# Four norm factors of a two-layer decoder kernel: from per-column sums and a spreading product to one product with a matrix of ones

## The chip, the cores and the metric

The kernel runs on 1 core of one Trainium2 chip. The metric is the time of one execution on the device in microseconds (us); smaller is better. The chip gave the kernel before 2523.98 us as the median of 3 runs (2523.86 to 2524.05). Beside these runs there is one profiled execution, whose trace is read here; L-numbers in it are lines of the kernel before.

## The reference

A decoder with two layers works on a residual stream h of 256 tokens by 2048 features in float32. Layer 0 has a dilated sliding-window attention, layer 1 a sparse attention with shared keys and values. What surrounds the change is the second half of each layer:

```python
def rmsnorm(x, g):
    xf = x.astype(jnp.float32)
    y = xf * lax.rsqrt(jnp.mean(xf * xf, axis=-1, keepdims=True) + NORM_EPS)
    return (y * g.astype(jnp.float32)).astype(x.dtype)

for i in range(DEPTH):                      # DEPTH = 2
    hn = rmsnorm(h, attn_norm_g[i])
    h = h + attention_i(hn)                 # two different mixers
    hn = rmsnorm(h, mlp_norm_g[i])
    h = h + jnp.square(jax.nn.relu(hn @ mlp_w1[i])) @ mlp_w2[i]
    gate = jax.nn.sigmoid(rmsnorm(h, ple_norm_g[i]) @ ple_w_gate[i])
    h = h + (p[i] @ ple_w_proj[i]) * gate
return rmsnorm(h, final_norm_g)
```

Every norm needs one number for each token: the reciprocal root of the mean square over 2048 features. The change is about how this number is made for four of the seven norms: the one before the MLP and the one before the gate, in both layers.

## The kernel before

**Tiles.** The stream is kept feature-major: 16 tiles `x[k]` of 128 features (partitions) by 256 tokens (columns). A product's stationary operand is a block of a weight matrix, its moving operand a tile of the stream. float32 accuracy is had from products of rounded parts: a weight chunk `raw` (128x1024 float32, 512 KB) is loaded by SP (L184), rounded to float32r by ScalarE (`whi`, L196), and what the rounding left is made by VectorE (`wlo`, L202). The stream's tiles are split in the same way into 512 columns: 256 of the rounded part, 256 of the rest. `mm_tile` then issues two products for a block of weights: `whi` with all 512 columns (L318) and `wlo` with the first 256 (L319).

**Order.** The order of all engines is written out by hand. `Program.run` goes over the weight chunks. For each chunk it issues the load up to seven chunks ahead (4 buffers of `raw`), the rounding four ahead (6 buffers of `whi`), the rest `wlo` three ahead (5 buffers); then it lets each open generator take one step (`advance`); then it issues the chunk's products; then it starts what has yielded the word `"tensor"`, which so stands behind the chunk's products. A `quad` is eight chunks that fill four PSUM banks (512 features of the output); a chunk in it is eight pairs of products. Two groups of four banks are used in turn, `mm` and `at`.

**The norm's factor.** The squares of the 16 tiles are summed into `acc` (128 partitions by 256 tokens). What is left is to sum `acc` over the partitions, and to have the result's reciprocal root on all 128 partitions, since it scales tiles whose partitions are features. `Norm.factor` starts behind chunk 4 of the first quad that uses the norm (`hooks`) and takes four steps:

- `column` (L234): for each half of the tokens a product with `acc` as stationary operand and one column of ones as moving operand. It gives the sums with tokens on partitions, 128x2.
- `root` (L240, L241): mean and epsilon on VectorE, the square root on ScalarE, both 128x2.
- `invert` (L247 to L253): a reciprocal, three operations that refine it, and two that multiply the identity with it, which gives `diag` (128x256). All on VectorE.
- `spread` (L257): a float32 product of a matrix of ones with `diag`, which puts the factors on all partitions; ScalarE copies them from PSUM to `sr` (L273).

Four norms go that way in the first quad of `mlp` (layers 0 and 1, scaled by `sr` at L461) and of the gate's quads in `ple` (L522). The norms before the two attentions use the same function with `roped=True`, and they also need the 128x2 column; the final norm calls `column`, `root`, `invert` and `spread` directly.

Of the kernel before, what the change touches and what calls it, by code (L numbers as in the profile page):

```python
# [10 lines left out]
F32 = mybir.dt.float32  # L11
F32R = mybir.dt.float32r
AF = mybir.ActivationFunctionType
ALU = mybir.AluOpType

P = 128
D = 2048
T = 256
KT = D // P
DH = 128  # L20
EPS = 1e-6
# [18 lines left out]
def f32(ap):  # L40
    return ap.bitcast(F32)
# [90 lines left out]
def kernel(ctx: ExitStack, tc: tile.TileContext, a: dict, out: bass.AP):  # L132
    nc = tc.nc
# [3 lines left out]
    const = ctx.enter_context(tc.tile_pool(name="const", bufs=1))  # L137
    xpool = ctx.enter_context(tc.tile_pool(name="x", bufs=1))
    stat = ctx.enter_context(tc.tile_pool(name="stat", bufs=2))
    tmp = ctx.enter_context(tc.tile_pool(name="tmp", bufs=2))  # L140
# [4 lines left out]
    cur = {}  # L145
# [10 lines left out]
    def bank():  # L156
        return pspool.tile([P, 512], F32, tag="mm", name="mm", bufs=4)

    def banks2():
        return pspool.tile([P, 2, 512], F32, tag="at", name="at", bufs=2)  # L160
# [5 lines left out]
    x = [xp[k // 2][:, k % 2 * T:(k % 2 + 1) * T] for k in range(KT)]  # L166
    ones = const.tile([P, P], F32, name="ones")
    nc.vector.memset(ones, 1.0)
    ident = const.tile([P, P], F32, name="ident")
    ropeC = const.tile([32, T], F32, name="ropeC")  # L170
    ropeS = const.tile([32, T], F32, name="ropeS")
# [34 lines left out]
    class Norm:  # L206
# [49 lines left out]
        def spread(self, ps):  # L256
            nc.tensor.matmul(ps[:, 128:128 + T], ones, self.diag, start=True, stop=True)  # L257
            return ps[:, 128:128 + T]

        def factor(self, roped=False):  # L260
            while self.done < KT:
                yield
            yield "tensor"
            ps = self.column([self.acc])
            yield
            self.root(ps)
            yield
            self.invert()
            yield "tensor"
            rp = self.spread(ps)  # L270
            yield
            r = stat.tile([P, T], F32, tag="sr", name="sr", bufs=1)
            nc.scalar.copy(r, rp)  # L273
            if roped:
                yield
                self.rc = stat.tile([P, T], F32, tag="rc", name="rc", bufs=1)
                self.rs = stat.tile([32, T], F32, tag="rs", name="rs", bufs=1)
                nc.vector.tensor_mul(self.rs, r[:32, :], ropeS)
                nc.vector.tensor_copy(self.rc, r)
                nc.vector.tensor_mul(self.rc[:32, :], r[:32, :], ropeC)  # L280
            self.r = r
# [39 lines left out]
    def sum_halves(ps):  # L321
        s = tmp.tile([P, T], F32, tag="es", name="es", bufs=4)
        nc.scalar.copy(s, ps[:, :T])  # L323
        t = tmp.tile([P, T], F32, tag="et", name="et", bufs=7)
        nc.vector.tensor_add(t, ps[:, T:], s)  # L325
        return t

    parity = [0]
# [123 lines left out]
    def mlp(layer, xg, norm, to, norm2):  # L452
        for b in range(NFB):
            h = [None] * 16
            for q in range(4):
                def done(f, ps, q=q, h=h):
                    t = sum_halves(ps)
                    yield
                    while norm.r is None:
                        yield  # L460
                    nc.vector.scalar_tensor_tensor(t, t, 0.0, norm.rb, op0=ALU.max, op1=ALU.mult)  # L461
                    yield
                    nc.scalar.activation(t, t, AF.Square)
                    ht = cur["h"].tile([P, 2 * T], F32R, tag="h", name="h", bufs=20)
                    yield from split_to(ht, t)
                    h[4 * q + f] = ht
                base = layer * 128 + (b * 4 + q) * 8
                quad(lambda c, base=base: a["w1"][base + c], KT, xg, done,
                     {4: [norm.factor]} if b == 0 and q == 0 else None, late=True)
            for q in range(4):  # L470
                def done(f, ps, q=q, b=b):
                    k = 4 * q + f
                    add_to_x(k, ps)
                    if b == NFB - 1:
                        yield
                        yield from renorm(k, G_PLE + layer, to, norm2)
                base = layer * 128 + (b * 4 + q) * 8
                quad(lambda c, base=base: a["w2"][base + c], 16, h, done, late=True)
# [10 lines left out]
    def ple(layer, pg, xg, norm, nxt, norm2, last):  # L489
        pj = [None] * KT  # L490

        def last_gate(ps):

            k = KT - 1
            prog.until(lambda: norm2.done == k)
            t = tmp.tile([P, T], F32, tag="et", name="et", bufs=7)
            nc.vector.tensor_mul(t, ps[:, :T], norm.rb)
            nc.scalar.activation(t, t, AF.Sigmoid)
            nc.scalar.activation(warm, ones[:, :1], AF.Sqrt)
            nc.vector.tensor_mul(t, t, pj[k])  # L500
            nc.vector.tensor_add(x[k], x[k], t)
            s = norm2.square(k, nc.vector)
            col = norm2.column([norm2.acc, s])
            norm2.root(col)
            nc.scalar.activation(x[k], x[k], AF.Identity, scale=gains[:, G_FIN, k:k + 1])
            norm2.invert()
            r = norm2.spread(col)
            for i, (k0, n) in enumerate([(0, 1), (1, 1)] + [(2 * j, 2) for j in range(1, KT // 2)]):
                y = xp[k0 // 2][:, k0 % 2 * T:(k0 % 2 + n) * T]
                y3 = y.rearrange("p (n t) -> p n t", t=T)  # L510
                nc.vector.tensor_mul(y3, y3, r[:, None, :].to_broadcast([P, n, T]))
                (nc.sync, nc.scalar)[i % 2].dma_start(out[:, k0 * T:(k0 + n) * T], y)
            return
            yield

        def gate_done(k, ps):
            t = sum_halves(ps)
            for _ in range(k % 4 // 2):
                yield
            while norm.r is None:  # L520
                yield
            nc.vector.tensor_mul(t, t, norm.rb)  # L522
            yield
            nc.scalar.activation(t, t, AF.Sigmoid)
            yield
            nc.vector.tensor_mul(t, t, pj[k])
            nc.vector.tensor_add(x[k], x[k], t)
            yield
            if last or k < 12:
                s = norm2.square(k)  # L530
                if last:
                    nc.scalar.activation(x[k], x[k], AF.Identity, scale=gains[:, G_FIN, k:k + 1])
                yield
                norm2.add(s)
            else:
                yield from renorm(k, G_KV, nxt, norm2)

        for q in range(4):
            def proj_done(f, ps, q=q):
                s = tmp.tile([P, T], F32, tag="es", name="es", bufs=4)  # L540
                nc.scalar.copy(s, ps[:, :T])
                t = cur["h"].tile([P, T], F32, tag="pj", name="pj", bufs=8)
                nc.vector.tensor_add(t, ps[:, T:], s)
                pj[4 * q + f] = t
                return
                yield
            quad(lambda c, q=q: a["w_proj"][layer * 4 + q], 2, pg, proj_done)
            hooks = {4: [norm.factor]} if q == 0 else {}
            if q == 3 and not last:
                for c in range(6):  # L550
                    hooks[c] = [lambda k=k: split_x(k, G_KV, nxt) for k in (2 * c, 2 * c + 1)]
            if q == 3 and last:
                for f in range(4):
                    single(lambda c, f=f: a["w_gl"][2 * f + c], xg,
                           (lambda ps, k=12 + f: gate_done(k, ps)) if f < 3 else last_gate,
                           ring=lambda: banks2()[:, 0, :], one_half=f == 3)
            else:
                quad(lambda c, q=q: a["w_gate"][layer * 32 + q * 8 + c], KT, xg,
                     lambda f, ps, q=q: gate_done(4 * q + f, ps), hooks)
# [21 lines left out]
    def start_x(k):  # L581
        return split_x(k, G_ATTN, x_a0)
# [117 lines left out]
    hooks = {c: [lambda k=k: start_x(k) for k in (2 * c + 2, 2 * c + 3)] for c in range(7)}  # L700
# [3 lines left out]
    for h in range(HA):  # L704
        for i in range(6):
            single(lambda c, h=h, i=i: a["w_qk"][(h * 6 + i) * 2 + c], x_a0,
                   lambda ps, h=h, i=i: qk_done(h, i, ps),
# [418 lines left out]
    for h in range(HB):  # L1126
# [4 lines left out]
        if h:  # L1131
            prog.op(lambda h=h: b_scores(h - 1))
    hooks = {0: [lambda: b_pv(HB - 4, True), lambda: b_transpose(HB - 3)],
             1: [lambda: b_scores(HB - 1, banks2)],
             2: [lambda: b_pv(HB - 3, True), lambda: b_transpose(HB - 2)],
             4: [lambda: b_pv(HB - 2, True), lambda: b_transpose(HB - 1)],
             5: [lambda: b_pv(HB - 1, True)]}
# [107 lines left out]
```

## Time and profile before

| | |
|---|---|
| median of 3 runs | 2523.98 us |
| profiled execution | 2523.56 us |
| its span, first to last instruction | 2521.8 us |
| TensorE (PE) busy | 2502.3 us, 99% of the span |
| VectorE (DVE) busy | 1719.2 us, 68% |
| ScalarE (ACT) busy | 1339.7 us, 53% |
| GpSimd (POOL) busy | 10.4 us |
| granted TensorE clock, mean | 0.998 |
| read from HBM | 461.65 MB, 184 GB/s over the span |

The span leaves out 1.8 us of the profiled execution's time, which lies around the first and last instruction. PE is TensorE's products, PEld its weight loads, which overlap the products. A product's row in the trace runs until its modelled end, and the next one starts before that; what a product costs TensorE is read from one start to the next.

### The profile page before, as it was taken

The page shows a single profiled execution, that of the slowest core. Times are in us where ns is not written, and L with a number is a line of the kernel's source. Part 1 is how long each engine was busy: PE and PEld are TensorE (multiplying, and loading weights), DVE is VectorE, ACT ScalarE, POOL GpSimd, SP SyncE. Part 2 cuts the span into 40 slices and gives each one's busy share as a digit, 9 for nine tenths or more (in the row PEclk, how much of TensorE's full clock was granted, in tenths as well). Part 3 has the DMA queues.
Part 4 walks back from the last instruction along what each step waited for, and adds up shares of the span by engine and source line. Part 5 has one row for each costly group of instructions (what it writes and reads, how often), then busy time and mean ns, then how long its engine had stood idle before and what let it go on. Part 6 is the DMA issues. An engine that isn't in the chain of part 4 may idle for free.

```text
span 2521.8 us, 37917 instructions
## 1 busy us (share of the span) xinstructions
PE 2502.3 (99%) x14399; PEld 2198.0 (87%) x14399; DVE 1719.2 (68%) x3005; ACT 1339.7 (53%) x2146; POOL 10.4 (0%) x24
## 2 busy tenths in 40 slices
PE   9999999999999999999999999999999999999997
PEld 7888888888888888888888889888888888888887
DVE  6766677866566665567787989776656556556777
ACT  6444444554354453455564788655435445445555
POOL 0000000000000000000000000000000000000000
PEclk9999999999999999999999999999999999999999
DMA  7555555566666666566566754456666666666663
GB/s 265 175 177 180 172 164 177 176 187 191 189 189 191 192 187 191 191 190 187 186 198 191 243 159 125 142 189 186 191 191 189 189 190 191 190 189 191 191 185 118
DMA packets 129831, 466.23 MB, mean 185 GB/s; under 512 B 14576, under 2 KB 15600, under 8 KB 129648
## 3 DMA queue, kind: packets, MB, share of 16 engines
q1 hardware_dynamic: 128400, 461.76, 58.7%
q8 instruction: 113, 1.85, 0.3%
q0 software_dynamic: 528, 1.07, 0.2%
q10 hardware_dynamic: 720, 0.98, 0.1%
q14 instruction: 70, 0.57, 0.1%
HBM read 461.65 MB, written 2.10 MB: 184 GB/s over the span
## 4 chain that ended last, share of the span: by engine, by line
PE 99%; DVE 1%; DMA 0%; issue 0%; ACT 0%; SPq 0%; DVEq 0%
PE mm L318 31%; PE at L318 26%; PE mm L319 16%; PE at L319 13%; PE mm L403 1%; PE mm L401 1%; PE mm L402 1%; PE at L401 1%; PE at L402 1%; PE at L403 1%; PE at L1092 0%; PE at L635 0%; PE mm L1116 0%; PE mm L855 0%; PE mm L856 0%; PE mm L688 0%
## 5 line engine op out<-in xcount | busy, mean ns | idle before, releaser
L202 DVE TENSOR_TENSOR wlo<-raw,whi 128x1024 fp32r<-128x1024 f32 (+1 forms) x874 | 1065.1, 1220 | 623.6 <-PE at L319 242.1
L196 ACT CAST whi<-raw 128x1024 fp32r<-128x1024 f32 (+1 forms) x874 | 920.3, 1054 | 914.6 <-PE at L318 407.7
L318 PE MATMUL mm<-xa,whi 128*128 128x512 f32 x2176 | 766.4, 396 | 0.0
L319 PE MATMUL mm<-xa,wlo 128*128 128x256 f32 x2176 | 608.8, 280 | 0.0
L318 PE MATMUL at<-xa,whi 128*128 128x512 f32 x1648 | 573.6, 392 | 0.0
L318 PEld LDWEIGHTS mm<-xa,whi 128*128 128x128 f32 x2176 | 407.9, 187 | 92.6 <-issue 0.4
L319 PE MATMUL at<-xa,wlo 128*128 128x256 f32 x1648 | 461.1, 280 | 0.0
L319 PEld LDWEIGHTS mm<-xa,wlo 128*128 128x128 f32 x2176 | 410.8, 189 | 0.4
L318 PEld LDWEIGHTS at<-xa,whi 128*128 128x128 f32 x1648 | 308.3, 187 | 68.0
L318 PE MATMUL mm<-h,whi 128*128 128x512 f32 x1024 | 355.7, 391 | 0.0
L318 PE MATMUL at<-h,whi 128*128 128x512 f32 x1024 | 355.7, 391 | 0.0
L319 PEld LDWEIGHTS at<-xa,wlo 128*128 128x128 f32 x1648 | 311.3, 189 | 0.1
L319 PE MATMUL mm<-h,wlo 128*128 128x256 f32 x1024 | 286.7, 280 | 0.0
L319 PE MATMUL at<-h,wlo 128*128 128x256 f32 x1024 | 286.7, 280 | 0.0
L318 PEld LDWEIGHTS at<-h,whi 128*128 128x128 f32 x1024 | 191.5, 187 | 42.0
L318 PEld LDWEIGHTS mm<-h,whi 128*128 128x128 f32 x1024 | 191.5, 187 | 42.0
L319 PEld LDWEIGHTS mm<-h,wlo 128*128 128x128 f32 x1024 | 193.5, 189 | 0.0
L319 PEld LDWEIGHTS at<-h,wlo 128*128 128x128 f32 x1024 | 193.5, 189 | 0.0
L325 DVE TENSOR_TENSOR et<-mm,es 128x256 f32<-128x256 f32 x137 | 55.7, 421 | 83.0 <-ACT es L323 80.9
L323 ACT COPY es<-mm 128x256 f32<-128x256 f32 x137 | 48.3, 371 | 67.5 <-PE mm L319 64.6
L325 DVE TENSOR_TENSOR et<-at,es 128x256 f32<-128x256 f32 x103 | 43.4, 422 | 36.7 <-ACT es L323 31.2
L323 ACT COPY es<-at 128x256 f32<-128x256 f32 x103 | 37.7, 370 | 51.8 <-DVE et L325 40.3
(292 smaller groups left out, 2372.3 us busy)
## 6 DMA issues: line engine op xcount, KB each, us to landing
raw<-in_w SPq DMA_DIRECT2D x512, 512.0 KB, 3.5
raw<-in_w_qk SPq DMA_DIRECT2D x96, 512.0 KB, 3.6
raw<-in_w_gate SPq DMA_DIRECT2D x56, 512.0 KB, 3.6
raw<-in_w_kv SPq DMA_DIRECT2D x48, 512.0 KB, 4.2
raw<-in_w_v SPq DMA_DIRECT2D x47, 512.0 KB, 3.6
raw<-in_w_q SPq DMA_DIRECT2D x32, 512.0 KB, 4.3
raw<-in_w_oB SPq DMA_DIRECT2D x32, 512.0 KB, 3.6
raw<-in_w_oA SPq DMA_DIRECT2D x16, 512.0 KB, 3.6
```

What stands on the lines that cost most here:

```text
L196: nc.scalar.copy(hi[:, c], t[:, c])
L202: nc.vector.tensor_sub(lo[:, c], t[:, c], f32(hi)[:, c])
L318: nc.tensor.matmul(ps, hi[:, col:col + P], rhs, start=first, stop=False)
L319: nc.tensor.matmul(ps[:, :T], lo[:, col:col + P], rhs[:, :T], start=False, stop=last)
L323: nc.scalar.copy(s, ps[:, :T])
L325: nc.vector.tensor_add(t, ps[:, T:], s)
L401: nc.tensor.matmul(st[j], xh, wh, start=k == 0, stop=False)
L402: nc.tensor.matmul(st[j], xl, wh, start=False, stop=False)
L403: nc.tensor.matmul(st[j], xh, wl, start=False, stop=k == KT - 1)
```

## The change

A new generator `factor_rows` takes the place of `factor` for the four norms. ScalarE rounds `acc` to float32r, VectorE makes what is left, and both stand beside each other in one tile of 512 columns, taken from the ring of the MLP's `h` tiles. One product with a float32r matrix of ones as stationary operand sums both parts over the partitions, and gives the sums on all partitions at once. The mean, root, reciprocal and refinement are then done on 128x256 instead of 128x2. `diag`, the second product and the copy to `sr` fall away. The matrix of ones is written once by GpSimd at the start.

```diff
     ones = const.tile([P, P], F32, name="ones")
     nc.vector.memset(ones, 1.0)
+    onesr = const.tile([P, P], F32R, name="onesr")
+    nc.gpsimd.memset(f32(onesr), 1.0)
...
+        def factor_rows(self):
+
+            while self.done < KT:
+                yield
+            a = cur["h"].tile([P, 2 * T], F32R, tag="h", name="h", bufs=20)
+            nc.scalar.copy(a[:, :T], self.acc)
+            yield
+            nc.vector.tensor_sub(a[:, T:], self.acc, f32(a[:, :T]))
+            yield "tensor"
+            ps = banks2()[:, 0, :] if parity[0] else bank()
+            nc.tensor.matmul(ps, onesr, a, start=True, stop=True)
+            yield
+            v, z = (tmp.tile([P, T], F32, tag="et", name="et", bufs=7) for _ in range(2))
+            r = stat.tile([P, T], F32, tag="sr", name="sr", bufs=1)
+            nc.vector.tensor_scalar(z, ps[:, :T], 1.0 / D, EPS, op0=ALU.mult, op1=ALU.add)
+            nc.vector.scalar_tensor_tensor(v, ps[:, T:], 1.0 / D, z, op0=ALU.mult, op1=ALU.add)
+            nc.scalar.activation(z, v, AF.Sqrt)
+            yield
+            nc.vector.reciprocal(r, z)
+            nc.vector.tensor_mul(z, r, r)
+            nc.vector.scalar_tensor_tensor(z, z, -0.5, v, op0=ALU.mult, op1=ALU.mult)
+            nc.vector.scalar_tensor_tensor(r, z, 1.5, r, op0=ALU.add, op1=ALU.mult)
+            self.r = r
...
                 quad(lambda c, base=base: a["w1"][base + c], KT, xg, done,
-                     {4: [norm.factor]} if b == 0 and q == 0 else None, late=True)
+                     {4: [norm.factor_rows]} if b == 0 and q == 0 else None, late=True)
...
-            hooks = {4: [norm.factor]} if q == 0 else {}
+            hooks = {4: [norm.factor_rows]} if q == 0 else {}
```

## The prediction

> **What bounds the kernel now.** The page comes first: span, busy shares, and the chain that ended last.
>
> ```profile
> span 2521.8 us, 37917 instructions
> PE 2502.3 (99%) x14399; PEld 2198.0 (87%) x14399; DVE 1719.2 (68%) x3005; ACT 1339.7 (53%) x2146; POOL 10.4 (0%) x24
> PE 99%; DVE 1%; DMA 0%; issue 0%; ACT 0%; SPq 0%; DVEq 0%
> ```
>
> The chain is TensorE's own queue from end to end: the time is the sum of what its products cost, and the other engines count only where TensorE has to wait for them. So the next question is whether it waits around the four norms. The table of stretches, 20 us around each of the four, answers it (its columns: stretch, its length, then PE, PEld, DVE, ACT and POOL busy):
>
> ```profile
> 497.00:517.00 20.00, 20.00 (x117) 17.52 (x116) 11.98 (x24) 9.95 (x14) 0.00 (x0) 1.00 0.57 184
> 1211.00:1231.00 20.00, 20.00 (x117) 17.55 (x117) 11.16 (x21) 7.83 (x11) 0.00 (x0) 1.00 0.64 194
> 1699.00:1719.00 20.00, 20.00 (x117) 17.51 (x116) 11.96 (x24) 10.01 (x15) 0.00 (x0) 1.00 0.63 186
> 2413.00:2433.00 20.00, 20.00 (x118) 17.55 (x117) 11.17 (x20) 7.68 (x12) 0.00 (x0) 1.00 0.65 201
> ```
>
> PE is busy in all 20.00 us of each, at the full granted clock (1.00), while VectorE has 8 to 9 us free and ScalarE 10 to 12. There is no stall to take away. What can be gained is TensorE time of removed products; what can be lost is TensorE time of the new product, or a wait that the longer work on VectorE creates.
>
> **What is removed from TensorE.** A busy row overlaps the next one, so I go from start to start, in the timeline of PE. First the norm before the first MLP:
>
> ```profile
> 505.75 0.28 PE L319 MATMUL mm<-xa,wlo 128*128 128x256 f32 x1
> 505.86 0.50 PE L234 MATMUL at<-ones,acc 128*128 128x1 f32 x4
> 506.22 0.48 PE L318 MATMUL mm<-xa,whi 128*128 128x512 f32 x1
> 506.54 0.28 PE L319 MATMUL mm<-xa,wlo 128*128 128x256 f32 x1
> 506.66 0.40 PE L318 MATMUL mm<-xa,whi 128*128 128x512 f32 x1
> 506.89 0.28 PE L319 MATMUL mm<-xa,wlo 128*128 128x256 f32 x1
> ...
> 511.86 0.39 PE L318 MATMUL mm<-xa,whi 128*128 128x512 f32 x1
> ...
> 514.63 0.59 PE L257 MATMUL at<-diag,ones 128*128 128x256 f32 x2
> 514.88 0.59 PE L318 MATMUL at<-xa,whi 128*128 128x512 f32 x1
> 515.30 0.28 PE L319 MATMUL at<-xa,wlo 128*128 128x256 f32 x1
> 515.42 0.39 PE L318 MATMUL at<-xa,whi 128*128 128x512 f32 x1
> 515.65 0.28 PE L319 MATMUL at<-xa,wlo 128*128 128x256 f32 x1
> ```
>
> An undisturbed product of 512 float32r columns takes 506.89 - 506.66 = 0.23 us, one of 256 takes 0.11 to 0.12 (506.66 - 506.54). `column` is two float32 products, run as two passes each (the x4). From its start to the start of the second product behind it are 506.54 - 505.86 = 0.68 us; the 512-column product in between would take 0.23, so `column` costs 0.45 us, part of it as delay of its successor. `spread`, one float32 product of 256 columns in two passes, in the same way: 515.30 - 514.63 = 0.67, less 0.23, 0.44 us. Together 0.89 us. The last of the four norms gives the same: 2422.58 - 2421.89 = 0.69 and 2431.49 - 2430.82 = 0.67, less 0.23 each, 0.90 us.
>
> ```profile
> 2421.89 0.50 PE L234 MATMUL mm<-ones,acc 128*128 128x1 f32 x4
> 2422.26 0.48 PE L318 MATMUL at<-xa,whi 128*128 128x512 f32 x1
> 2422.58 0.28 PE L319 MATMUL at<-xa,wlo 128*128 128x256 f32 x1
> ...
> 2430.82 0.59 PE L257 MATMUL mm<-diag,ones 128*128 128x256 f32 x2
> 2431.07 0.58 PE L318 MATMUL mm<-pg,whi 128*128 128x512 f32 x1
> 2431.49 0.28 PE L319 MATMUL mm<-pg,wlo 128*128 128x256 f32 x1
> ```
>
> For four norms I take 4 x 0.885 = 3.54 us.
>
> **What is added to TensorE.** One float32r product, 128x128 weights, 512 columns, between chunks 5 and 6. Its nearest row is L318, which has the same shape and type: 0.23 us. The other end is what a float32 product costs in the same place, delay of the successor included: 0.44 (`spread`). Below, it cannot go under nothing. I take 0.23, because nothing but its operands' names differs from L318: 4 x 0.23 = 0.92 us. Net gain: 3.54 - 0.92 = 2.62 us; with the dear end 3.54 - 1.76 = 1.78; with a free product 3.54.
>
> The Trainium skill, "Perfetto Trace Analysis", section Engine Utilization, halves the array's output rate for FP32_LOW_HIGH. If the two passes are that mode, `spread` should cost twice the 0.115 us of 256 float32r columns, 0.23 us, and four norms would gain 4 x (0.45 + 0.23 - 0.23) = 1.8 us; the row says 0.44, nearly four times, and I go by the row.
>
> **What the new work on VectorE and ScalarE costs.** Here are the rows of VectorE and ScalarE around the first of the four, and the prices of the operations:
>
> ```profile
> 506.12 1.23 DVE L202 TENSOR_TENSOR wlo<-raw,whi 128x1024 fp32r<-128x1024 f32 x1 [1.61 <-PE mm L319]
> 507.26 0.15 DVE L240 TENSOR_SCALAR sv<-at 128x2 f32<-128x2 f32 x1
> 509.34 1.23 DVE L202 TENSOR_TENSOR wlo<-raw,whi 128x1024 fp32r<-128x1024 f32 x1 [1.93 <-ACT sz L241]
> 510.49 0.16 DVE L247 RECIPROCAL sy<-sz 128x2 f32<-128x2 f32 x1
> 511.26 0.48 DVE L253 TENSOR_SCALAR diag<-ident,col 128x128 f32<-128x128 f32 x2
> 512.12 1.22 DVE L202 TENSOR_TENSOR wlo<-raw,whi 128x1024 fp32r<-128x1024 f32 x1 [0.36 <-issue]
> ...
> 507.01 1.28 ACT L241 ACT_TABLE_LOAD   x1
> 509.17 1.05 ACT L196 CAST whi<-raw 128x1024 fp32r<-128x1024 f32 x1 [0.66 <-PE mm L318]
> 511.99 1.05 ACT L196 CAST whi<-raw 128x1024 fp32r<-128x1024 f32 x1 [1.76 <-PE mm L318]
> ```
>
> ```profile
> L247 DVE RECIPROCAL sy<-sz x7: 155/158/167, 57.3 to 2510.4; 128x2 f32<-128x2 f32 x7
> L1073 DVE RECIPROCAL sums<-sums x16: 191/191/194, 1479.5 to 1608.9; 128x6 f32<-128x6 f32 x16
> L461 DVE SCALAR_TENSOR_TENSOR et<-et,sr x128: 412/417/421, 517.7 to 2321.4; 128x256 f32<-128x256 f32 x128
> L218 ACT ACTIVATE sq<-x 128x256 f32<-128x256 f32 x89 | 36.3, 409 | 14.3 <-DVE acc L226 8.1 <-DVE x L527 6.1
> ```
>
> Six new 128x256 operations on VectorE at 0.42 us (L461) are 2.5 us. No row has a reciprocal of 256 columns. The two that exist grow by (191 - 158) / 4 = 8.25 ns a column, so I estimate 0.158 + 254 x 0.00825 = 2.25 us; the far end, all of 158 ns for two columns, would be 79 ns a column or 20.2 us, the near end an ordinary 0.42. I take 2.25, since the slope separates the fixed part from the columns. So 4.8 us of VectorE for each norm, where some 1.4 us fall away.
>
> Who waits? Product by product, with times of before. The generator begins behind chunk 4, so ScalarE's copy of `acc` stands behind a rounding well ahead, and VectorE's subtraction behind the `wlo` of chunk 8, one before the row at 506.12: `a` is ready at about 505. The product stands behind chunk 5; a chunk is 514.63 - 511.86 = 2.77 us, so it starts at about 509.1 and does not wait. It ends by 509.5; mean and sum of the halves on VectorE until 510.3; the root on ScalarE (0.41 as L218, its table loaded meanwhile at 507.01, as before) until 510.75. Behind the root waits the rounding that was at 509.17: 1.6 us late. The `wlo` at 509.34 moves to 510.3; reciprocal and three operations then run from 511.5 to 515.0, and the `wlo` at 512.12, queued behind them, ends at 516.2 instead of 513.34: 2.9 us late.
>
> That one belongs to chunk 11, whose products start three chunks into the next quad, at 514.88 + 0.19 (the delay behind `spread`) + 3 x 2.77 = 523.4. It was 10.0 us early and is still 7 us early. Its `raw` buffer comes free 2.9 us later too, so SP issues the load for chunk 15 later; that chunk is needed 11 us after chunk 11, and its load, rounding and subtraction would start at 516.2, 18 us ahead. So the longer VectorE block is hidden by the three chunks of lead.
>
> The factor itself is ready at 515.0; its first user, L461, ran at 517.7. One of the four steps is gone, so `sr` comes no later than the copy that ScalarE made behind `spread`. The bank of the sums is read by 510.3, before the next quad needs it. The `h` ring only turns by one tile; its 20 hold 16 and four that are long consumed. GpSimd's write of the ones lies at the start, hundreds of us before its use, and POOL is idle (0.00) around the norms. All this I cost at nothing; if the cover were gone, each norm would pay what exceeds 10 us of delay.
>
> **The sum.** From the profiled execution: 2523.56 - 2.62 = 2520.94, span 2519.2. The median before lies 0.42 above it, so the forecast for the median is 2523.98 - 2.62 = 2521.4 us, 0.10% less. A measurement of this kernel can tell about 0.2%, 5.0 us, from no change: by that bound the forecast is "within".
>
> **Rivals.** *The product is dear* (0.44 us, a switch of product type or its semaphores): gain 1.8, 2522.2 us. For it: the successor of each float32 product is delayed. Against: L318 and L319 alternate without any delay. Chance 0.11.
>
> *No gain*: TensorE's removed time was cover for something that ends at the same moment, 2523.9 us. Against: PE 20.00 of 20.00 and a chain that is 99% PE. The same result if the new product waits 0.65 us in each norm, for a subtraction that I place 4 us ahead. Chance 0.05.
>
> *Slower: the reciprocal on full rows holds the weights up.* In place of the lead, `wlo` of chunk 11 comes late. It decides from 10 us of delay, so from a reciprocal of about 9.3 us, or 36 ns a column; at 79 ns a column the delay is 2.9 + 18.0 = 20.9 us, each norm stalls 10.9, and the time is 2521.4 + 43.6 = 2565.0 us. For it: only 2 and 6 columns are in the trace. Against: their slope is a fourth of that point. Chance 0.04.
>
> *Faster by over 0.2%*: more than 5.0 us, though all that the four norms cost TensorE is 3.54. It would need waits elsewhere to go, of which I see none in this part. Chance 0.03.
>
> **Numbers.** TensorE's weight loads are now and then held up for 0.4 us by nothing that the table of waits can name:
>
> ```profile
> PEld mm L318 <- issue: 0.4, 1, 0.4
> ```
>
> With fewer instructions ahead, such hiccups may fall elsewhere; I allow two, 0.8 us. The forecast has 0.77. The range reaches from a free product, 2523.98 - 3.54 = 2520.4, past the dear product (2522.2) by these 0.8, to 2523.0; that holds forecast and first rival, 0.88. Within 0.2% are forecast, dear product and no gain, 0.93; faster 0.03; slower 0.04.
>
> **What would show it.** In the trace after: the product of 512 columns between chunks 5 and 6, its successor 0.23 us behind it; no float32 product in the first quad; reciprocals of about 2.25 us; the `wlo` behind them some 3 us late, and PE still 20.00 of 20.00. Wrong would be: a PE wait for `h` or `wlo` in these stretches, a successor 0.4 us behind the product, or a span that falls by other than about 2.6 us.

## The result, and the profile after

The changed kernel takes 2551.82 us (median of 4 runs, 2551.09 to 2552.28) against 2524.02 us before on the same chip: 27.8 us slower, a ratio of 1.0109 with a 95% interval of 1.0097 to 1.0121. The forecast was 2521.4 us. Its profiled execution took 2551.48 us, with these first lines of the page:

```profile
span 2549.7 us, 37875 instructions
PE 2529.5 (99%) x14379; PEld 2198.1 (86%) x14379; DVE 1731.5 (68%) x3005; ACT 1341.0 (53%) x2146; POOL 10.7 (0%) x25
PE 98%; DVE 1%; ACT 0%; issue 0%; DMA 0%; SPq 0%; DVEq 0%
```

TensorE has 20 products fewer and is busy 27 us longer. It is not waiting: around the four norms PE is still busy in every microsecond (table of stretches), and the table of waits names none of them.

```profile
497.00:517.00 20.00, 20.00 (x115) 17.32 (x114) 15.44 (x25) 11.11 (x16) 0.00 (x0) 1.00 0.50 159
1225.00:1245.00 20.00, 20.00 (x115) 17.33 (x114) 13.97 (x21) 8.08 (x13) 2.67 (x7) 1.00 0.62 193
1715.00:1735.00 20.00, 20.00 (x115) 17.33 (x115) 15.44 (x25) 10.39 (x15) 0.00 (x0) 1.00 0.55 180
2442.00:2462.00 20.00, 20.00 (x116) 17.33 (x115) 13.97 (x21) 8.08 (x13) 0.00 (x0) 1.00 0.57 183
```

```profile
PE at L427 <- ACT whi L198: 6.6, 1, 6.6
PE at L236 <- DVE sq L222: 2.2, 1, 2.2
PE at L259 <- DVE diag L255: 1.8, 1, 1.8
```

(These three lie at the start and the end of the program and were there before, the first at 6.0 us.) The new product itself costs what was forecast:

```profile
508.82 0.29 PE L345 MATMUL mm<-xa,wlo 128*128 128x256 f32 x1
508.95 0.39 PE L272 MATMUL at<-h,onesr 128*128 128x512 f32 x1
509.18 0.40 PE L344 MATMUL mm<-xa,whi 128*128 128x512 f32 x1
509.41 0.28 PE L345 MATMUL mm<-xa,wlo 128*128 128x256 f32 x1
```

509.18 - 508.95 = 0.23 us, its successor undisturbed (0.23). The loss is elsewhere, in stretches whose instructions the change does not touch. Four stretches of 100 us inside the two MLPs, first of the kernel before, then of the kernel after; behind PE's busy time stands the number of products that fall into it:

```profile
600.00:700.00 100.00, 100.00 (x579) 88.19 (x578) 59.10 (x78) 41.37 (x47) 0.00 (x0) 1.00 0.60 190
1000.00:1100.00 100.00, 100.00 (x579) 88.19 (x578) 61.72 (x86) 50.21 (x72) 0.00 (x0) 1.00 0.61 190
1800.00:1900.00 100.00, 100.00 (x579) 88.19 (x578) 58.69 (x76) 40.27 (x44) 0.00 (x0) 1.00 0.61 190
2200.00:2300.00 100.00, 100.00 (x579) 88.19 (x578) 61.06 (x84) 48.94 (x69) 0.00 (x0) 1.00 0.62 190
```

```profile
600.00:700.00 100.00, 100.00 (x569) 86.74 (x568) 58.09 (x75) 39.12 (x41) 0.00 (x0) 1.00 0.59 188
1000.00:1100.00 100.00, 100.00 (x568) 86.67 (x568) 57.11 (x75) 45.15 (x59) 0.00 (x0) 1.00 0.58 185
1800.00:1900.00 100.00, 100.00 (x569) 86.67 (x568) 59.05 (x78) 40.71 (x46) 0.00 (x0) 1.00 0.59 188
2200.00:2300.00 100.00, 100.00 (x568) 86.70 (x568) 57.90 (x77) 42.55 (x52) 0.00 (x0) 1.00 0.58 185
```

Busy time and granted clock (1.00) are the same; 579 products have become 568 or 569. Taken from start to start over runs of 32 pairs, a pair of products (512 and 256 columns) takes 346.7 ns before and 353.3 ns after, everywhere in both MLPs. I call these two values the fast and the slow cadence. Inside such a stretch PE's busy time cannot show the difference; PEld's shows it (88.2 against 86.7 us). The Trainium skill, "Trainium Kernel Development and Optimization", section Performance Expectations, calls matmul busy time a bad metric for how close a kernel is to roofline, and the busy share of weight loads a good one. The trace agrees on which of the two tells these kernels apart: busy time is 100.00 in both, the weight loads have 88.2 and 86.7.

The kernel before already had both cadences. Here is its second norm; the first row of each two-row group starts 22 pairs ahead of the second:

```profile
1220.29 0.40 PE L318 MATMUL at<-xa,whi 128*128 128x512 f32 x1
1228.06 0.40 PE L318 MATMUL at<-xa,whi 128*128 128x512 f32 x1
...
1229.20 0.40 PE L318 MATMUL mm<-pg,whi 128*128 128x512 f32 x1
1236.84 0.39 PE L318 MATMUL at<-xa,whi 128*128 128x512 f32 x1
```

Between `column` and `spread` a pair took 7.77 / 22 = 353 ns, behind `spread` 7.64 / 22 = 347. Each of the four old factors left the fast cadence behind it. The new factor does not: the stream comes into the first quad of the MLP in the slow one (353 ns from its first products at 492 on, in both kernels) and stays in it until the next old-style factor, the one before layer 1's attention, at 1340.9, and from 1725.6 almost to the end. That is 832 + some 800 us, of which (353.3 - 346.7) / 353.3 = 1.87% is lost: 30.5 us. Less the 2.6 us of saved products it is 27.9; measured were 27.8.

### The profile page after: what moved, and what is told of

The parts are those of the page before. It is cut to its first block, busy times and chain, and to the rows that moved or that the text cites. A ratio compares the mean times of both kernels' runs of the same rounds, so it can differ in the third digit from the quotient of the medians.

```text
span 2549.7 us, 37875 instructions
## 1 busy us (share of the span) xinstructions
PE 2529.5 (99%) x14379; PEld 2198.1 (86%) x14379; DVE 1731.5 (68%) x3005; ACT 1341.0 (53%) x2146; POOL 10.7 (0%) x25
## 4 chain that ended last, share of the span: by engine, by line
PE 98%; DVE 1%; ACT 0%; issue 0%; DMA 0%; SPq 0%; DVEq 0%
PE mm L344 32%; PE at L344 26%; PE mm L345 16%; PE at L345 13%; PE mm L429 1%; PE mm L428 1%; PE mm L427 1%; PE at L427 1%; PE at L428 1%; PE at L429 1%; PE at L1118 0%; PE at L661 0%; PE mm L1142 0%; PE mm L714 0%; PE at L1070 0%; ACT whi L198 0%
## 5 line engine op out<-in xcount | busy, mean ns | idle before, releaser
L344 PE MATMUL at<-xa,whi 128*128 128x512 f32 x1648 | 582.9, 398 | 0.0
L344 PE MATMUL mm<-h,whi 128*128 128x512 f32 x1024 | 362.5, 399 | 0.0
L344 PE MATMUL at<-h,whi 128*128 128x512 f32 x1024 | 362.5, 399 | 0.0
```

Source lines behind the costliest of these rows:

```text
L344: nc.tensor.matmul(ps, hi[:, col:col + P], rhs, start=first, stop=False)
```

## The experiments

Theory A: TensorE runs the stream of pairs in one of two cadences, and what the old float32 products did beside their work was to leave it in the fast one. The rivals: B, the change moved tiles in memory (the ones matrix moves all later tiles, the sum's tile turns the ring of `h`); C, any extra product shifts the cadence.

**A float32 product behind the new factor.** The kernel after, with one more product at the place of the old `spread`:

```diff
             nc.vector.scalar_tensor_tensor(r, z, 1.5, r, op0=ALU.add, op1=ALU.mult)
             self.r = r
+            yield "tensor"
+            nc.tensor.matmul(ps[:, :T], ones, self.acc, start=True, stop=True)
+            yield
```

> The kernel after, plus one float32 product of ones with the squares' sum (256 columns, two passes, result unused) behind chunk 7 of each of the four first quads, where the old spread stood. Theory A (cadence): TensorE runs the same pair of products in one of two cadences, 346.7 ns or 353.3 ns; whatever products the 128x256 float32 product of the old spread left behind ran in the fast one, and the new factor has no such product, so both MLPs stay in the slow one. Then this run returns to 346.7 ns from the second quad on: 2521.4 + 4 x 0.44 + some 0.3 for the slow pairs before it = about 2523.5 us. Theory B (placement: the ones matrix moves every later tile by 512 bytes and the sum's tile turns the ring of h by one): nothing moves back, pairs stay at 353.3 ns, 2551.8 + 1.8 = 2553.6 us. Theory C (any extra product shifts the cadence): near A as well.

Measured: 2523.06 us (ratio to before 0.9994, 0.9983 to 1.0005). The added product and two 100 us stretches, from timeline and table of stretches:

```profile
514.67 0.59 PE L286 MATMUL at<-acc,ones 128*128 128x256 f32 x2
514.92 0.58 PE L347 MATMUL at<-xa,whi 128*128 128x512 f32 x1
```

```profile
600.00:700.00 100.00, 100.00 (x579) 88.19 (x578) 59.09 (x78) 41.33 (x47) 0.00 (x0) 1.00 0.63 190
1800.00:1900.00 100.00, 100.00 (x579) 88.19 (x578) 58.71 (x76) 40.65 (x44) 0.00 (x0) 1.00 0.63 190
```

579 products again. Work was added, 28.8 us went away. All that the change moved, its longer VectorE block included, is still in this kernel, so none of it costs the time by itself.

**Placement alone.** The kernel before with the float32r ones, the tile from `h` and the split written but unused:

```diff
+    onesr = const.tile([P, P], F32R, name="onesr")
+    nc.gpsimd.memset(f32(onesr), 1.0)
...
+            a = cur["h"].tile([P, 2 * T], F32R, tag="h", name="h", bufs=20)
+            nc.scalar.copy(a[:, :T], self.acc)
+            yield
             ps = self.column([self.acc])
+            nc.vector.tensor_sub(a[:, T:], self.acc, f32(a[:, :T]))
```

> The kernel before, with the float32r ones, the tile from the ring of h and both parts of the split written (ScalarE's copy and VectorE's subtraction, read by nothing), but with the old products. Theory A (cadence): 2524.0 us, pairs at 346.7 ns. Theory B (placement): about 2551 us, pairs at 353.3 ns in the MLPs.

Measured: 2524.06 us (ratio 1.0000, 0.9989 to 1.0012), 579 products in 600 to 700 us. B falls.

**A second float32r product behind the new factor.**

```diff
+            yield "tensor"
+            nc.tensor.matmul(ps, onesr, a, start=True, stop=True)
+            yield
```

> The kernel after, plus a second copy of its float32r product (512 columns, one pass, result unused) behind chunk 7, where the first extra run has a float32 product. Theory A (cadence, float32 passes needed): pairs stay at 353.3 ns, 2551.8 + 4 x 0.23 = 2552.7 us. Theory C (any extra product shifts the cadence): 346.7 ns from there on, about 2522.6 us. Theory B (placement): 2552.7 us.

Measured: 2549.57 us, ratio 1.0100 (1.0070 to 1.0129). In the MLPs nothing changed, but in the gate stage of layer 0 (1250 to 1290 us) there are as many products as in the kernel before (233; the kernel after has 229 there):

```profile
600.00:700.00 100.00, 100.00 (x568) 86.70 (x567) 57.80 (x74) 39.08 (x41) 0.00 (x0) 1.00 0.62 187
1250.00:1290.00 40.00, 40.00 (x233) 35.28 (x232) 31.98 (x52) 23.59 (x39) 0.00 (x0) 1.00 0.68 202
```

Both gate stages turned fast, which is the 3.1 us below A's 2552.7. So a float32r product can change the cadence too; what A said of float32 passes being needed is too narrow, and C too wide.

**In one norm only.** The float32 product of the first experiment, but only in layer 0's MLP:

```diff
+            if self is n_m0:
+                yield "tensor"
+                nc.tensor.matmul(ps[:, :T], ones, self.acc, start=True, stop=True)
+                yield
```

> The kernel after, plus the float32 product of 256 columns behind chunk 7, but only in the first of the four norms (layer 0, before the MLP). If a cadence once taken lasts until a float32 product or a change of the pattern ends it, layer 0 runs at 346.7 ns a pair through MLP and gate stage, and layer 1 stays at 353.3 ns: about half of the loss is left, 2522 + 2320 pairs x 6.7 ns = about 2537.5 us. If the cadence only held near the product, about 2551 us. If the float32r product of the second norm threws layer 0's gate stage into the slow one, 2 us more.

Measured: 2536.92 us, ratio 1.0050 (1.0032 to 1.0069). Half of the loss is left, and the two layers' MLPs differ in one run:

```profile
600.00:700.00 100.00, 100.00 (x579) 88.15 (x579) 58.87 (x77) 40.87 (x45) 0.00 (x0) 1.00 0.61 190
2200.00:2300.00 100.00, 100.00 (x568) 86.67 (x567) 57.66 (x76) 45.94 (x60) 0.00 (x0) 1.00 0.60 187
```

One product of 0.44 us decides over more than 700 us of others. It was followed by the second norm's float32r product, and the stretch 1250 to 1290 held 233 products: here that product left the fast cadence standing.

**Which products set which cadence.** Three runs of the kernel before with 124 extra products each, behind chunks 3 and 6 of the MLPs' quads, kinds shuffled:

```diff
+    def probe(acts):
+        kind = order.pop(0)
+        n = int(kind[1:])
+        ps = banks2()[:, 0, :] if parity[0] else bank()
+        if kind[0] == "F":
+            nc.tensor.matmul(ps[:, :n], ones, f32(onesr)[:, :n], start=True, stop=True)
+        else:
+            nc.tensor.matmul(ps[:, :n], onesr[:, :P], acts[0][:, :n], start=True, stop=True)
```

> The kernel before with 124 extra products, one behind chunk 3 and one behind chunk 6 of every quad of both MLPs but the first of each: six kinds in a shuffled order, float32 of 1, 128 or 256 columns (two passes each) and float32r of 128, 256 or 512 columns (one pass); weights are ones, results unused. What counts is the pitch of the pairs between one extra product and the next. If float32 products of 256 columns set the fast cadence, every stretch behind one is at 346.7 ns whatever stood before, and stretches behind float32r of 512 columns keep the cadence that stood before. If instead any product can throw the stream from one cadence to the other, both kinds show 346.7 and 353.3 behind them. No stretch should lie between the two but where it changes.

> The same 124 extra products in another shuffled order. A rule on kinds that holds in the first order has to hold here: float32 of 256 columns leaves 346.7 ns behind it, from both cadences; what the other kinds leave behind should depend on the kind and the cadence before it, and on nothing else, if the kind is what decides.

> The kernel before with 124 extra products as in the two runs with shuffled kinds, six other kinds: float32 of 192 and of 512 columns, float32r of 384 columns, two float32r of 512 columns in a row, two float32r of 256 columns in a row, and two float32 of one column (the shape of the old column products). If what resets the cadence is the long delay of the successor behind a wide float32 product, float32 of 512 and of 192 columns leave 346.7 ns behind them from both cadences, as 256 did in 41 of 41 cases, and the float32r kinds do not. If 256 columns in float32 is a coincidence of lengths, 192 and 512 leave both cadences behind them.

They took 2566.99, 2567.46 and 2580.89 us, one execution each; only their cadences are read here. The third run had doubled products as well, and took the float32 columns from the same tile as the others. One float32r and one float32 product of the first run, each with a stretch before and behind it: 19 pairs lie between the first two and the last two rows of each block, except 15 pairs between the last two of the first block:

```profile
528.83 0.39 PE L320 MATMUL at<-xa,whi 128*128 128x512 f32 x1
535.42 0.40 PE L320 MATMUL at<-xa,whi 128*128 128x512 f32 x1
535.77 0.39 PE L347 MATMUL mm<-xa,onesr 128*128 128x512 f32 x1
536.70 0.40 PE L320 MATMUL at<-xa,whi 128*128 128x512 f32 x1
542.00 0.40 PE L320 MATMUL mm<-xa,whi 128*128 128x512 f32 x1
...
917.31 0.40 PE L320 MATMUL mm<-xa,whi 128*128 128x512 f32 x1
924.02 0.40 PE L320 MATMUL mm<-xa,whi 128*128 128x512 f32 x1
924.38 0.59 PE L345 MATMUL at<-onesr,ones 128*128 128x256 f32 x2
925.16 0.40 PE L320 MATMUL mm<-xa,whi 128*128 128x512 f32 x1
931.75 0.39 PE L320 MATMUL at<-xa,whi 128*128 128x512 f32 x1
```

6.59 / 19 = 347 ns before the float32r product of 512 columns, 5.30 / 15 = 353 behind it; 6.71 / 19 = 353 before the float32 product of 256, 6.59 / 19 = 347 behind. Over all 372 stretches the last twelve pairs average 346.6 or 346.7 ns in 219 cases and 353.3 in 153; nothing lies between. Sorted by the cadence before the product, and that of up to 16 pairs behind it:

| extra product | was fast: then fast / slow | was slow: then fast / slow |
|---|---|---|
| float32, 192 columns | 19 / 0 | 2 / 0 |
| float32, 256 columns | 14 / 0 | 27 / 0 |
| float32, 512 columns | 17 / 0 | 3 / 0 |
| float32, 128 columns | 10 / 11 | 7 / 13 |
| float32, 1 column | 12 / 7 | 8 / 15 |
| two float32 of 1 column | 16 / 1 | 1 / 2 |
| float32r, 512 columns | 2 / 25 | 1 / 13 |
| float32r, 384 columns | 14 / 6 | 1 / 0 |
| float32r, 256 columns | 6 / 11 | 13 / 11 |
| float32r, 128 columns | 4 / 14 | 9 / 15 |
| two float32r of 512 columns | 13 / 5 | 3 / 0 |
| two float32r of 256 columns | 16 / 0 | 1 / 4 |

Float32 products of 192 columns and more were followed by the fast cadence in 82 of 82 cases, from both sides. A float32r product of 512 columns, the shape that the change puts in, was followed by the slow one in 38 of 41: it does not only fail to reset, it threw a fast stream out in 25 of 27 cases. The other kinds are followed by both, and the kind alone does not decide. The doubled kinds met the slow cadence in 11 cases between them, too few for a rule by kind and cadence alone.

The same traces show what else decides. They hold starts in whole nanoseconds, and in these the fast cadence has two forms: every pair takes 347 ns, or pairs of 343 and 350 alternate. The slow one repeats a group of three, 349, 350 and 361. The rows' own lengths show the three forms too (line, count, then shortest, median and longest in ns; kernel before, the even form first, then the slow one, then the alternating one):

```profile
L318 PE MATMUL at<-xa,whi x27: 391/391/391, 1209.8 to 1218.8; 128*128 128x512 f32 x27
L318 PE MATMUL at<-xa,whi x21: 395/398/403, 1220.6 to 1227.7; 128*128 128x512 f32 x21
L318 PE MATMUL mm<-xa,whi x19: 392/392/395, 507.7 to 513.9; 128*128 128x512 f32 x19
```

Sort the 372 cases by kind, by form, and by the place in the repeating group at which the product falls: of the 60 combinations that occur (50 of them more than once), none was followed by both cadences. A float32r product of 512 columns that met the alternating form was followed by the slow cadence in 25 of 25 cases; one that met the even form, by the fast one in 2 of 2. The 20 products of that kind in the kernel after and in the first, third and fourth experiments follow the same sorting, 20 of 20. This sorting was found in runs made for other questions; no run was made to test it.

**The new product in two halves.**

```diff
-            nc.tensor.matmul(ps, onesr, a, start=True, stop=True)
+            for j in range(2):
+                nc.tensor.matmul(ps[:, :T], onesr, a[:, j * T:(j + 1) * T], start=j == 0, stop=j == 1)
...
-            nc.vector.tensor_scalar(z, ps[:, :T], 1.0 / D, EPS, op0=ALU.mult, op1=ALU.add)
-            nc.vector.scalar_tensor_tensor(v, ps[:, T:], 1.0 / D, z, op0=ALU.mult, op1=ALU.add)
+            nc.vector.tensor_scalar(v, ps[:, :T], 1.0 / D, EPS, op0=ALU.mult, op1=ALU.add)
```

> The kernel after with its product in two float32r products of 256 columns that add up in one bank (one operation less on VectorE). By the shuffled runs a single float32r product of 256 columns leaves either cadence behind it, about evenly. If only wide float32 products reset, each of the four norms may fall on either side: between 2521.3 us (all fast) and 2551 us (all slow), in steps of about 13.7 us for an MLP. If the loss belonged to the width of 512 alone, 2521.3 us.

Measured: 2549.24 us, ratio 1.0096 (1.0067 to 1.0126): both MLPs slow (568 products from 600 to 700 us), both gate stages fast. The width of 512 was not the whole cause either.

**One float32 product in place of all.** No split and no ones in float32r; the rest of the new factor stays:

```diff
-            a = cur["h"].tile([P, 2 * T], F32R, tag="h", name="h", bufs=20)
-            nc.scalar.copy(a[:, :T], self.acc)
-            yield
-            nc.vector.tensor_sub(a[:, T:], self.acc, f32(a[:, :T]))
             yield "tensor"
             ps = banks2()[:, 0, :] if parity[0] else bank()
-            nc.tensor.matmul(ps, onesr, a, start=True, stop=True)
+            nc.tensor.matmul(ps[:, :T], ones, self.acc, start=True, stop=True)
...
-            nc.vector.tensor_scalar(z, ps[:, :T], 1.0 / D, EPS, op0=ALU.mult, op1=ALU.add)
-            nc.vector.scalar_tensor_tensor(v, ps[:, T:], 1.0 / D, z, op0=ALU.mult, op1=ALU.add)
+            nc.vector.tensor_scalar(v, ps[:, :T], 1.0 / D, EPS, op0=ALU.mult, op1=ALU.add)
```

> The new factor without the split: one float32 product of ones with the squares' sum (256 columns, two passes) in the place where the old column products stood, then the 128x256 root and reciprocal. No ones in float32r, no tile from the ring of h. Theory A (cadence): a float32 product of 256 columns leaves the fast cadence behind, so 2524.0 - 4 x (0.89 - 0.44) = about 2522.2 us. Theory B (placement): also 2522.2, since nothing is moved. If the cadence is set by what the two old products make together, some of the four norms leave the slow one: about 13.7 us more for each MLP in it, 1.9 for each gate stage.

> The run with one float32 product of 256 columns for each of the four norms and no split, once more, in more rounds: 2524.0 - 4 x (0.89 - 0.44) = 2522.2 us by the cost of the products alone, a ratio to the kernel before of 0.9993, if both run in the fast cadence from the first quad of each MLP on. By the first single round of it, 2521.9.

Measured: 2521.88 us in the first (ratio 0.9990, 0.9978 to 1.0001), 2521.54 us (11 runs, 2521.21 to 2522.76) in the second, against 2524.25 us of the kernel before beside it; ratio 0.9990, 0.9981 to 0.9999. It is the only version here whose interval lies wholly below the kernel before, if only just, and the gain is about what the products cost:

```profile
506.69 0.59 PE L266 MATMUL at<-acc,ones 128*128 128x256 f32 x2
506.93 0.58 PE L337 MATMUL mm<-xa,whi 128*128 128x512 f32 x1
507.35 0.28 PE L338 MATMUL mm<-xa,wlo 128*128 128x256 f32 x1
```

507.35 - 506.69 - 0.23 = 0.43 us for each norm, where the old factor had 0.89. It does the summing and the resetting in one.

## Why the prediction was wrong

**Removed products, 0.89 us a norm, and the added one, 0.23: right.** The added one is in the rows above. The removed ones agree with the float32-only version: it should gain 4 x (0.89 - 0.43) = 1.8 us and gained 2.7, with an interval of 0.3 to 4.8 by its ratio.

**The step that failed is the sum.** "There is no stall to take away. What can be gained is TensorE time of removed products" took the time of every other product as fixed, so that the change could only add or take away rows. The pairs that follow, some 4,600 of them, each became 6.6 ns longer: 30.5 us, where the sum has no term for them. The rows were there: I read the pair's pitch as "undisturbed" from one place (506.66 to 506.89), behind a float32 product, and did not compare it with the rows ahead of it. In the kernel before, the pitch changed at each of the four factors.

**VectorE and ScalarE: right in kind.** Their rows after:

```profile
510.30 0.42 ACT L278 ACTIVATE et<-et 128x256 f32<-128x256 f32 x1 [1.75 <-DVE et L277]
```

```profile
511.31 1.75 DVE L280 RECIPROCAL sr<-et 128x256 f32<-128x256 f32 x1
514.01 0.42 DVE L283 SCALAR_TENSOR_TENSOR sr<-et,sr 128x256 f32<-128x256 f32 x1
514.36 1.22 DVE L204 TENSOR_TENSOR wlo<-raw,whi 128x1024 fp32r<-128x1024 f32 x1
517.29 0.76 DVE L487 SCALAR_TENSOR_TENSOR et<-et,sr 128x256 f32<-128x256 f32 x2
```

The root began at 510.30 (forecast 510.3), the reciprocal took 1.75 us (2.25), the factor was ready at 514.4 (515.0), before its first user at 517.29, and the `wlo` behind it ended at 515.6, 2.2 us late (2.9), with no wait of TensorE. The rival with a slow reciprocal (chance 0.04) named the right side and the wrong mechanism; no rival had a change in the pace of the other products.

**The price of float32 columns: right by the row.** A float32 product of 256 columns cost 0.43 to 0.44 us here, against 0.115 for float32r. The half rate of the Trainium skill, "Perfetto Trace Analysis", section Engine Utilization, would give 0.23, if the two passes are the mode it means; the measurement decides.

**What the prediction said would show it wrong** did: a span that moves by other than 2.6 us, with PE at 20.00 of 20.00. Its other two signs, a wait of PE for `h` or `wlo` and a successor 0.4 us behind the new product, did not appear.

What in TensorE makes the cadences stays open; the traces give their forms only. Nor are two cadences the whole of it: in the projection ahead of the first MLP, pairs of the same two shapes ran at 349 ns in the kernel before (20.93 us for 60 pairs from 457.89 on).

## What to carry to other kernels

Where one engine is the bound and never waits, read the pitch of its repeated work in several places, ahead of and behind each instruction that a change removes, and not only that instruction's cost: the count of instructions in equal stretches shows at once what busy time hides. Before a rare product of another type is taken out of a long even stream, put it back alone behind the change; if that gives the time back, its side effect was worth more than its cost. Here a float32 product of 192 columns or more was such a one, and the best version kept it as the summing product.

## What the runs showed of the hardware that was not expected

The same pair of products of 512 and 256 float32r columns ran at 346.7 or 353.3 ns at a granted clock of 1.00, with nothing between in 372 stretches, and held one cadence for over 700 us. Float32 products of 192 to 512 columns set the fast one in 82 of 82 cases; float32r products of 512 columns were followed by the slow one in 38 of 41. Kind, form and place in the repeating group together sorted all 372 cases without a mixed one. A reciprocal of 256 columns took 1.75 us, less than the slope between 2 and 6 columns gave (2.25).
